# A hybrid decoder block on eight cores: two passes over 512 tokens, or one pass over 1024 with the MLP in two phases

## Chip, cores, metric

One Trainium2 chip, all 8 cores. Each core handles 1024 of the 8192 tokens with all the weights; nothing passes between cores. The metric is device microseconds of the slowest core for one execution. Most executions agree within 0.3%. Some fall in a second, slower state: the four cores of a die (0 to 3 or 4 to 7), or both dies, show a lower granted TensorE clock, and the time is longer. An execution is called slow when one die is over 1% longer than the other at a lower clock, or when it is over 1.5% above the quickest of its kernel. Here fast executions are compared with fast ones. Traces are of fast executions, or of a core on a die that was not disturbed, and then the text says so.

## The reference

```
D_MODEL 4096, BATCH 4, SEQ 2048, one layer;  CONV_WIDTH = GMLP_WIDTH = 2048;  D_FF 16384
xn = rmsnorm(x, mix_norm_g)
b, c, h_in, u, v = split(xn @ w_in)                    # w_in 4096 x 10240
y_a = b * causal_dwconv3(c * h_in)                     # 16 groups of 128 channels
y_b = gelu(u) * (tril(W_s) gelu(v) + bias)             # 16 heads, chunks of 128 positions
h   = x + [rmsnorm(y_a, ga), rmsnorm(y_b, gb)] @ w_out # w_out 4096 x 4096
h   = h + relu(rmsnorm(h, mlp_norm_g) @ w_up)^2 @ w_down   # 4096 x 16384 and back
out = rmsnorm(h, final_norm_g)
```

For one core that is 23,552 matmuls of 128x128 weights against 512 columns, if everything is 512 wide.

## The kernel before

It runs the whole layer twice, for 512 tokens each time, and reads all weights in each pass. The accumulator of 4 x 4096 floats a partition (`acc`) shares its memory with the temporaries of the two mixers. Operations go to per-engine queues, and a helper works out semaphore waits from the buffers that each one reads and writes.

```python
T = 512; NPASS = 2; NSLOT = 4                      # a weight tile: [128, 8192] bf16, 2 MB of bf16, 4 slots; f32 in DRAM

def nt(tt, slot, g_ap, g_buf, extra_w=()):          # norm of 128 tokens, then 32 transposes
    P.op("dve", scalar_tensor_tensor(out=xb, in0=acc[:, tt, :], scalar=stat[:, slot:slot + 1],
                                     in1=g_ap, op0=mult, op1=mult), ...)      # 128 x 4096
    for f4 in range(4):  P.pe([8 transposes of xb, bf16], ...)
    for f4 in range(4):  P.op("dve" or "act", copy psum -> x1, ...)

for ps_ in range(NPASS):
    ...                                             # load x, statistics, nt(): nothing else runs
    def ssq_mm(sq_ap, bsq, first, last):            # sum of squares over channels, for each 128 of them
        P.pe([lambda e: e.matmul(S_bank[:], lhsT=ones_f[:], rhs=sq_ap, start=first, stop=last)], ...)
    ...                                             # input projection + mixers, 20 groups of 256 columns
    P.fence(["sp"], all_tB)                         # acc is free only when the mixers are done
    for tt in range(NTT):
        P.dma("sp", s_x[tt], ... acc[:, tt, :] <- x[r0:r0 + 128, :], writes=B_acc[tt] + all_tB)
    for dc in range(8):                             # out-projection, added onto acc
        for half in range(2):
            slot, bslot = wtile(w_out[dc * 2 + half], v_out)
            ...
    for tt in range(NTT):  stats_fin(4 + tt)
    for tt in range(NTT):  nt(tt, 4 + tt, g2, bg2, ...)
    up_block(0)                                     # 16 blocks of 1024 hidden channels
    for fb in range(NFB):
        if fb + 1 < NFB:  up_block(fb + 1)          # relu, square -> aT in SBUF
        down_block(fb)                              # acc += psum, tensor_tensor on DVE
    ...                                             # final norm, store
# ... (cuts everywhere; operations written short)
```

## Time and profile before

The first three executions took 5658.6, 5661.7 and 5664.6 us; the median is 5661.7. The profiled execution has a span of 5616.7 us.

| stage (slowest core) | us | of it TensorE works |
|---|---|---|
| start of pass 0, start of pass 1 | 92 and 98 | 17 and 14 |
| input projection and mixers | 636 and 608 | nearly all |
| out-projection, with the wait for x before it and the norm after it | 301 and 301 | about 243 each |
| MLP | 1773 and 1775 | all |
| end | 31 | 0 |

Stage limits are the starts of the first large matmul of each kind in the chain of waits, so the stages add up to the span. The names of the engines in all lines: PE is TensorE (matmuls), PEld its weight loads, DVE VectorE, ACT ScalarE, POOL GpSimd, SP SyncE; PEclk is the granted TensorE clock. The lines below are from the page of the kernel before: busy time and share of each engine, three rows of the span cut into 40 slices (tenths), the weights' DMA queue (packets, MB, share), the chain that ended last, and groups of instructions (line, engine, operation, operands, shapes, count, then busy us, mean ns of one, and idle time before them with its cause).

```profile
span 5616.7 us, 62670 instructions; the slowest of 8 cores (5608.2 to 5616.7 us)
...
PE 5281.9 (94%) x25536; PEld 2427.1 (43%) x25536; DVE 1148.9 (20%) x1608; ACT 637.5 (11%) x1232; POOL 196.8 (4%) x374
...
PE   4999979799999999999949999889999999999997
...
PEclk9999989899999999999969999999999999999998
DMA  8887888688888888888589878876888888888885
...
q0 software_dynamic: 52992, 771.78, 77.7%
...
PE 92%; DMA 3%; DVE 3%; ACT 1%; issue 0%; SPq 0%; DVEq 0%; ACTq 0%
...
L660 PE MATMUL ps<-R,ws 128*128 128x512 bf16 x8192 | 1784.7, 379 | 3.0 <-ACT R L390 3.0
L681 PE MATMUL ps<-ws,R 128*128 128x512 bf16 x8192 | 1773.0, 379 | 0.0
...
L619 PE MATMUL ps<-ws,R 128*128 128x512 bf16 x2048 | 456.9, 387 | 55.0 <-DVE R L624 55.0
```

TensorE is busy 94% of the time and on 92% of the chain. L660 and L681 are the two MLP products. No idle time stands before L681, and 3 us before L660. The holes are in the slices: `4`, `7` and `8` at the start, about the middle, and where PEclk falls to 6. L619 is out-projection, with 55 us of idle time before it.

The next lines are stretches (from:to in us, length, busy time of each engine with its instructions, granted clock, DMA share, GB/s).

```profile
core 5: us, PE busy (x) PEld busy (x) DVE busy (x) ACT busy (x) POOL busy (x), PEclk, DMA share, GB/s
0.00:92.00 92.00, 17.14 (x176) 15.89 (x176) 36.98 (x38) 32.65 (x88) 4.75 (x10) 1.00 0.97 214
...
718.00:796.00 78.00, 43.19 (x168) 17.92 (x167) 7.73 (x8) 3.52 (x5) 1.58 (x3) 0.80 0.89 216
...
985.00:1030.00 45.00, 14.69 (x130) 13.56 (x131) 28.82 (x27) 7.05 (x9) 0.53 (x1) 0.58 0.37 87
1030.00:2803.00 1773.00, 1772.98 (x8191) 800.15 (x8189) 353.60 (x511) 173.31 (x318) 65.42 (x124) 1.00 0.82 148
2803.00:2901.00 98.00, 13.89 (x128) 13.04 (x128) 48.44 (x41) 27.18 (x76) 2.11 (x4) 0.53 0.77 226
```

The stretch 1030:2803 is pure matmul at full clock. The others are the losses: a start with 17 us of PE work in 92, a wait for the residual x (718:796), norm and transposes between out-projection and MLP (985:1030) at half the clock, and the start of pass 1.

### The profile page before, as it was taken

How to read it: one execution, taken by the hardware profiler on the slowest of the kernel's cores; microseconds unless marked ns; L12 is line 12 of the kernel's file. 1: busy time of each engine (PE TensorE's matmuls, PEld its weight loads, DVE VectorE, ACT ScalarE, POOL GpSimd, SP SyncE). 2: the span in 40 equal slices, each digit the busy share in tenths (PEclk: the TensorE clock that was granted, in tenths of full speed). 3: DMA queues.
4: the chain of work that ended last, by engine and by line, in shares of the span. 5: the costliest groups of instructions: out<-in, count | busy, mean ns of one | idle time of the engine just before them, and what ended most of it. 6: DMA issues, size and time to landing. Idle time of an engine off the chain costs nothing.

```text
span 5616.7 us, 62670 instructions; the slowest of 8 cores (5608.2 to 5616.7 us)
## 1 busy us (share of the span) xinstructions
PE 5281.9 (94%) x25536; PEld 2427.1 (43%) x25536; DVE 1148.9 (20%) x1608; ACT 637.5 (11%) x1232; POOL 196.8 (4%) x374
## 2 busy tenths in 40 slices
PE   4999979799999999999949999889999999999997
PEld 2444434344444444444424444344444444444443
DVE  2111112212212211221331111121221121122114
ACT  2111101100010001001121111011001000100011
POOL 0000000000000000000000000000000000000000
PEclk9999989899999999999969999999999999999998
DMA  8887888688888888888589878876888888888885
GB/s 180 135 136 129 140 174 154 117 153 153 150 152 152 153 153 152 154 150 152 104 215 159 145 130 146 173 141 128 153 153 152 150 152 152 153 153 152 153 150 135
DMA packets 68553, 840.87 MB, mean 150 GB/s; under 512 B 16690, under 2 KB 16690, under 8 KB 17202
## 3 DMA queue, kind: packets, MB, share of 16 engines
q0 software_dynamic: 52992, 771.78, 77.7%
q1 hardware_dynamic: 14708, 56.70, 3.0%
q10 hardware_dynamic: 576, 8.39, 0.4%
q8 instruction: 212, 3.47, 0.3%
q14 instruction: 65, 0.53, 0.0%
HBM read 1591.81 MB, written 16.78 MB: 286 GB/s over the span
## 4 chain that ended last, share of the span: by engine, by line
PE 92%; DMA 3%; DVE 3%; ACT 1%; issue 0%; SPq 0%; DVEq 0%; ACTq 0%
PE ps L660 32%; PE ps L681 31%; PE ps L459 20%; PE ps L619 7%; DMA R<-x 2%; DVE R L373 1%; PE ps L466 1%; PE ps L381 1%; DVE R L702 1%; DMA R<-mix_g 1%; PE ps L451 0%; DMA R<-xh 0%; DVE R L393 0%; DVE R L473 0%; ACT ps L346 0%
## 5 line engine op out<-in xcount | busy, mean ns | idle before, releaser
L660 PE MATMUL ps<-R,ws 128*128 128x512 bf16 x8192 | 1784.7, 379 | 3.0 <-ACT R L390 3.0
L681 PE MATMUL ps<-ws,R 128*128 128x512 bf16 x8192 | 1773.0, 379 | 0.0
L686 DVE TENSOR_TENSOR R<-ps,R 128x512 f32<-128x512 f32 x1024 | 708.6, 692 | 2843.9 <-PE ps L681 2843.9
L660 PEld LDWEIGHTS ps<-R,ws 128*128 128x128 bf16 x8192 | 799.5, 98 | 983.1 <-issue 5.4
L681 PEld LDWEIGHTS ps<-ws,R 128*128 128x128 bf16 x8192 | 801.5, 98 | 966.6
L459 PE MATMUL ps<-R,ws 128*128 128x512 bf16 x5120 | 1133.5, 380 | 3.4 <-ACT R L390 3.4
L459 PEld LDWEIGHTS ps<-R,ws 128*128 128x128 bf16 x5120 | 496.2, 98 | 621.0 <-issue 38.5
L619 PE MATMUL ps<-ws,R 128*128 128x512 bf16 x2048 | 456.9, 387 | 55.0 <-DVE R L624 55.0
L664 ACT ACTIVATE ps<-ps 128x512 f32<-128x512 f32 x256 | 149.0, 582 | 3004.6 <-PE ps L660 3004.6
L619 PEld LDWEIGHTS ps<-ws,R 128*128 128x128 bf16 x2048 | 203.4, 100 | 307.9 <-issue 75.8
L381 PE MATMUL ps<-ident_b,R 128*128 128x128 bf16 x512 | 56.8, 309 | 173.1 <-DVE R L373 173.1
L624 DVE SCALAR_TENSOR_TENSOR R<-ps,inv_tok,R 128x512 f32<-128x512 f32 x128 | 95.0, 750 | 417.8 <-PE ps L619 289.7
L666 ACT ACTIVATE R<-ps 128x512 bf16<-128x512 f32 x256 | 152.8, 597 | 23.9 <-ACT ps L664 0.7
L352 ACT ACTIVATE ps<-R 128x512 f32<-128x512 f32 x128 | 76.9, 601 | 653.9 <-DVE R L624 478.0
L506 DVE TENSOR_TENSOR R<-ps,R 128x512 f32<-128x512 f32 x32 | 22.1, 692 | 598.5 <-PE ps L459 598.5
L251 POOL DMA_DIRECT2D ws<-w_up x128 | 67.5, 527 | 1793.1 <-PE ps L681 1472.1
L381 PEld LDWEIGHTS ps<-ident_b,R 128*128 128x128 bf16 x512 | 53.0, 145 | 177.4 <-issue 177.4
L251 POOL DMA_DIRECT2D ws<-w_down x128 | 67.6, 528 | 1710.2 <-PE ps L660 1587.8
L251 POOL DMA_DIRECT2D ws<-w_in x80 | 42.4, 530 | 1296.5 <-PE ps L459 820.7
L565 DVE COPY R<-ps 128x512 bf16<-128x512 bf16 x32 | 13.6, 425 | 334.9 <-PE ps L561 334.9
L373 DVE SCALAR_TENSOR_TENSOR R<-R,stat 128x4096 bf16<-128x4096 f32 x16 | 71.7, 4481 | 14.0 <-DMA R<-mix_g 13.2
L466 PE MATMUL ps<-R,ones_f 128*128 128x512 f32 x128 | 68.3, 616 | 3.5 <-ACT R L586 3.5
(64 smaller groups left out, 682.0 us busy)
## 6 DMA issues: line engine op xcount, KB each, us to landing
ws<-w_up POOLq DMA_DIRECT2D x128, 2048.0 KB, 14.6
ws<-w_down POOLq DMA_DIRECT2D x128, 2048.0 KB, 14.5
ws<-w_in POOLq DMA_DIRECT2D x80, 2048.0 KB, 16.0
ws<-w_out POOLq DMA_DIRECT2D x32, 2048.0 KB, 15.4
R<-x SPq DMA_DIRECT2D x12, 2048.0 KB, 17.9
out<-R SPq DMA_DIRECT2D x8, 2048.0 KB, 8.5
R<-x ACTq DMA_DIRECT2D x4, 2048.0 KB, 17.4
R<-mix_g SPq DMA_DIRECT2D x2, 2048.0 KB, 32.4
```

The costliest lines, as they stand in the source:

```text
L251: P.dma("pool", s_slot[s], lambda e: e.dma_start(out=flat, in_=src_ap), writes=[B_slot[s]])
L373: P.op("dve", lambda e: e.scalar_tensor_tensor(out=xb, in0=src, scalar=stat[:, slot:slot + 1], in1=g_ap, op0=ALU.mult, op1=ALU.mult), read ...
L381: fns.append(lambda e, i=i, c=c, bank=bank: e.transpose(out=bank[:, i * 128:(i + 1) * 128], in_=xb[:, c * 128:(c + 1) * 128], identity=ide ...
L459: fns.append(lambda e, kc=kc, bank=bank: e.matmul(bank[:], lhsT=slot[:, kc, i * 128:(i + 1) * 128], rhs=x1[:, kc, 2:514], start=(kc == 0), ...
L466: P.pe([lambda e: e.matmul(S_bank[:], lhsT=ones_f[:], rhs=sq_ap, start=first, stop=last)], reads=[bsq, B_const], writes=[B_S])
L619: fns.append(lambda e, cc=cc, bank=bank, tt=tt, half=half, slot=slot: e.matmul(bank[:], lhsT=yT[:, half * 16 + cc, tt * 128:(tt + 1) * 128 ...
L624: P.op("dve", lambda e, bank=bank, dst=dst, tt=tt, half=half: e.scalar_tensor_tensor(out=dst, in0=bank[:], scalar=inv_tok[:, half * 4 + tt ...
L660: fns.append(lambda e, kc=kc, bank=bank, slot=slot, i=i: e.matmul(bank[:], lhsT=slot[:, kc, i * 128:(i + 1) * 128], rhs=x1[:, kc, 2:514], ...
L664: P.op("act", lambda e, bank=bank: e.activation(out=pst[3][:], in_=bank[:], func=AF.Relu), reads=[bb], writes=[B_ps[3]])
L666: P.op("act", lambda e, fb=fb, fcl=fcl: e.activation(out=aT[fb % 2][:, fcl, :], in_=pst[3][:], func=AF.Square), reads=[B_ps[3]], writes=[B ...
L681: fns.append(lambda e, fc=fc, bank=bank, slot=slot, tt=tt, dcl=dcl, fb=fb: e.matmul(bank[:], lhsT=aT[fb % 2][:, fc, tt * 128:(tt + 1) * 12 ...
L686: P.op("dve", lambda e, bank=bank, dst=dst: e.tensor_tensor(out=dst, in0=bank[:], in1=dst, op=ALU.add), reads=[bb, B_acc[tt][dc]], writes= ...
```

## The change

Its intent: read each weight once. All 1024 tokens stay in memory as the transposed activation `XT`. They are transposed *before* the norm, with the norm's gain applied as the psum (the memory that takes TensorE's results) is copied out. The token factor 1/rms, which only scales a column of the product, is multiplied in when the product is read. The first six products already run while x arrives ("k-outer"). The MLP becomes two phases: all of up, whose 33.5 MB of activations go to DRAM, then all of down. The factor for `relu(.)^2`, 1/ms, is applied as down is accumulated. h goes to DRAM and back since its memory is needed. Sums of squares are added up on DVE.

```diff
-T = 512 ... NPASS = 2 ... FB = 1024
+TOK = 1024
+NT = 8
+NFULL = 15
+        h_d = nc.dram_tensor("h_d", [8, 128, 4096], F32).ap()
+        a_d = nc.dram_tensor("a_d", [DFF // 128, 128, TOK], BF16).ap()
-        slots = [sb("ws%d" % i, [128, 8192], BF16) for i in range(NSLOT)]
+        slots = [sb("ws%d" % i, [128, 4096], BF16) for i in range(NSLOT)]
 ... # start: transposes of raw x in f32, and six products fed as blocks of x come in
+        for db in range(9):
+            for u in range(8):
+                if db < 8:
+                    ... P.pe(4 f32 transposes) ; evac_t(XT[...], bnk[:], g1[:, kc:kc + 1], ...)
+                    ... P.act(Square of xst, accum_out=statp[...])
+                if db > 0:
+                    kouter((db - 1) * 4 + u // 2, range((u % 2) * 3, (u % 2) * 3 + 3))
 ... # the token norm on the psum read
+            P.dve(lambda e: e.tensor_tensor(out=z, in0=bnk[:], in1=inv_bc[:, 2 + p * 512:514 + p * 512],
+                                            op=ALU.mult), reads=[bb, B_inv], writes=[bz])
 ... # c and h_in with their two halo columns: three pieces of 342 columns
+            for p in range(3):
+                bnk, bb = in_piece(sl, bsl, p * 342, 342)
 ... # sums of squares on DVE
-                P.pe([lambda e: e.matmul(S_bank[:], lhsT=ones_f[:], rhs=sq_ap, start=first, stop=last)], ...)
+                    P.dve(lambda e, sa=sa, sq_=sq_: e.tensor_tensor(out=sa, in0=sa, in1=sq_, op=ALU.add), ...)
 ... # out-projection: h is transposed in f32 among its matmuls and stored to DRAM
+                            defer(3, lambda db=db: x2_part(db, 0, (0, 1)))
+            P.dma("sp", s_hs[db % 2], ... h_d[db] <- a)
 ... # up, then down
+        for f in range(DFF // 128):
+            ... 2 x 32 matmuls, relu, square -> at
+            P.dma("sp", s_aT[f % 3], lambda e, f=f, at=at: e.dma_start(out=a_d[f], in_=at), ...)
+        for f in range(NFULL):
+            ... acc = psum * inv2m + acc  (scalar_tensor_tensor), a tile of 8 matmuls
+        ... # last 1024 channels in two halves, tiles of 4 matmuls, the second half with sums of squares and final norm
 ... # (cuts everywhere)
```

## The prediction

> **What bounds the kernel now.** TensorE. The page puts PE at 94% of the 5616.7 us span, and the chain of waits is 92% PE. In the two MLP stretches (windows 1030–2803 and 3811–5585) PE is busy 1773 of 1773 us at granted clock 1.00, 215.8 ns a 128x512 matmul in down and 217.1 in up (chain pieces 55.25 and 55.57 us for 256). That agrees with the Trainium skill, "TensorE: Matmul & The Clock Gate", section "Back-to-back issue gap" (N/2.4 + 2.5 ns = 215.8). DMA is 82% busy there but nothing waits for it. So weight traffic is not the bound; only the some 530 us outside the 23552 large matmuls (5083 us at 215.8) can be won.
>
> Where these lie (windows, chain, timeline): start of pass 0, 92 us; start of pass 1, 98; both without large matmuls. Wait for the residual x before out-projection, about 42 us twice (78 us windows with 168 matmuls). Norm and transposes between out-projection and MLP, 45 us twice at clock 0.58. Ones-matmuls in f32 for the sums of squares (L466), 64 x 0.87 = 56 us. Halo products (L451), 25 us. Norm extraction inside the input projection, 6 us twice. End, 31 us.
>
> **What the change does.**
> - Weights are read once, DMA bytes for weights halve (772 to 386 MB), about 100 MB of h and activations are added. Off the path: 0 us either way.
> - One start instead of two. 16.8 MB of x at the 214 GB/s of the first window, plus three weight tiles: about 110 us (estimate), but 192 matmuls (41 us) run inside it. Saves 120.
> - Residual x is loaded under the end of the conv stage and h goes out and back in the background: saves 84.
> - The norm moves onto the psum reads, x is transposed under out-projection: saves 90 less about 3 of bubble, but 256 f32 transposes are put between the matmuls, 0.11 to 0.22 us each (four took 1.09 us after an idle stretch, at L477): costs 28 to 56.
> - Ones-matmuls become DVE adds: saves 56. Halo columns go into 342-wide pieces: saves 25, and 1024 more matmul instructions of the conv stage cost some 4 us by the same 2.5 ns; DVE stays far below PE.
> - Up reads an aligned activation tile: it may run at 215.8 rather than 217.1 ns, 0 to 10 us.
> - End: the last half of down does 4-matmul tiles (0.86 us) with a square (0.8 us on ACT), an add (0.7 us on DVE), and the final norm; ACT and DVE become the limit, some 70 to 75 us of work against 55 of PE, then the last store. Tail about 33 us, no gain.
>
> **Sum of stages after (estimate):** start 110, gating heads 420, conv 672, out-projection 485, up 1770, down 1768, tail 33, bubbles 8: span 5266 to 5290. The time before lies 45 us above its span; so 5320 us.
>
> **Predicted: 5320 us, range 5280 to 5390.** Faster by over 2%: 0.96; within 2%: 0.03; slower: 0.01.
>
> **What would show it.** MLP stages still 3536–3547 us together with no PE gap and clock 1.00; no wait for x before out-projection; no stretch at clock 0.5 to 0.6 in mid-kernel; PE share about 97 to 98%; DMA share about 45%; conv stage about 670 us; start about 110 us; between out-projection and up a gap below 5 us; f32 transposes 60 us or less in out-projection.
>
> **What would make it wrong.** A lower granted clock under one unbroken dense stream. A start bound by the two transposing banks or by ACT squares rather than DMA (to 140 us). Costlier f32 transposes or switches between f32 and bf16 (another 50 us). Activations coming late from DRAM at the start of down. A tail above 50 us.

## The result, and the profile after

Six executions of the changed kernel: 5272.2, 5268.6 and 5267.6 us fast, 5520.7, 5723.8 and 5890.7 us slow. In the slow ones one die had a clock of 0.88 to 0.95 and the other ran its usual 5259 to 5268 us. The median of all six, 5396 us, says little about the kernel. The kernel before took 5640.5, 5660.3 and 5615.7 us in these rounds; with the first three that makes its first six. The ratio of fast runs to those of before was 0.9326 (95% interval 0.9282 to 0.937), on a later visit 0.9381 (0.9364 to 0.9397). Such a ratio is the mean time of one kernel's fast runs over that of the other's in the same rounds, so it is not quite the ratio of the medians that I quote.

So the kernel is 6 to 7% faster. The predicted 5320 us is 51 us too high, and the fast runs lie below the range (5280 to 5390); the median lies above it.

The same lines of the page, of the changed kernel (L803 is up, L843 down but for its last 1024 channels):

```profile
span 5270.5 us, 61915 instructions; the slowest of 8 cores (5257.8 to 5270.5 us)
...
PE 5179.0 (98%) x25401; PEld 2480.1 (47%) x25401; DVE 1250.5 (24%) x1706; ACT 619.9 (12%) x1144; POOL 241.5 (5%) x391
...
PE   6999999999999999999999999999999999999997
...
PEclk8999999999999999999999999999999999999998
DMA  6544434345555664444444444464444445444454
...
q0 software_dynamic: 54288, 385.90, 40.5%
...
PE 98%; another core or an unknown queue 0%; DMA 0%; issue 0%; DVE 0%; ACT 0%; POOLq 0%; DVEq 0%; ACTq 0%
...
L803 PE MATMUL ps<-AB,ws 128*128 128x512 bf16 x8192 | 1768.3, 379 | 0.0
L843 PE MATMUL ps<-ws,TT 128*128 128x512 bf16 x7680 | 1657.8, 379 | 0.0
```

TensorE is at 98%, and the slices show one hole only, the first. The weights' queue moved half the bytes. Stretches by stage, with the same columns; the last one starts where the tiles of 4 matmuls do:

```profile
0.00:130.40 130.40, 79.57 (x470) 53.85 (x471) 39.11 (x66) 55.36 (x153) 9.82 (x20) 0.90 0.68 171
...
1220.00:1692.80 472.80, 471.73 (x2321) 230.89 (x2320) 113.32 (x156) 74.17 (x173) 17.41 (x33) 1.00 0.54 132
1692.80:3460.90 1768.10, 1768.10 (x8193) 801.57 (x8192) 0.48 (x3) 313.56 (x512) 67.06 (x127) 1.00 0.51 104
3460.90:5118.50 1657.60, 1657.60 (x7682) 751.47 (x7680) 719.71 (x959) 1.23 (x2) 63.33 (x120) 1.00 0.49 100
5118.50:5270.50 152.00, 114.42 (x512) 50.24 (x510) 116.54 (x153) 61.50 (x144) 42.52 (x13) 0.91 0.53 160
```

| stage | before | after, predicted | after, measured | gained |
|---|---|---|---|---|
| start(s) | 190.6 | 110 | 130.4 | 60.2 |
| input projection, mixers | 1244.6 | 1092 | 1089.4 | 155.2 |
| out-projection and its gaps | 601.9 | 485 | 472.9 | 129.0 |
| MLP matmuls | 3548.3 | 3538 | 3536.2 | 12.1 |
| end | 31.3 | 33 | 41.5 | -10.2 |
| bubbles | in the stages | 8 | in the stages | |
| span | 5616.7 | 5266 | 5270.5 | 346.2 |

"End" after is the last stretch, 152.0 us, less its 512 matmuls at 215.8 ns (110.5 us). The predicted *span*, 5266 to 5290 us, holds the measured 5270.5. What failed is what I added to it.

### The profile page after: what moved, and what is told of

Same layout as the page of the kernel before. It is cut to its first block, busy times and chain, and to the rows that moved or that the text cites. A ratio compares the mean times of both kernels' runs of the same rounds, so it can differ in the third digit from the quotient of the medians.

```text
span 5270.5 us, 61915 instructions; the slowest of 8 cores (5257.8 to 5270.5 us)
## 1 busy us (share of the span) xinstructions
PE 5179.0 (98%) x25401; PEld 2480.1 (47%) x25401; DVE 1250.5 (24%) x1706; ACT 619.9 (12%) x1144; POOL 241.5 (5%) x391
## 4 chain that ended last, share of the span: by engine, by line
PE 98%; another core or an unknown queue 0%; DMA 0%; issue 0%; DVE 0%; ACT 0%; POOLq 0%; DVEq 0%; ACTq 0%
PE ps L803 34%; PE ps L843 31%; PE ps L531 20%; PE ps L744 8%; PE ps L865 2%; PE ps L436 1%; PE ps L449 1%; PE ps L726 1%; DMA AB<-x 0%; ACT TT L831 0%; PE ps L566 0%; PE ps L582 0%; DVE AB L826 0%; POOLq L925 0%
## 5 line engine op out<-in xcount | busy, mean ns | idle before, releaser
L803 PE MATMUL ps<-AB,ws 128*128 128x512 bf16 x8192 | 1768.3, 379 | 0.0
L843 PE MATMUL ps<-ws,TT 128*128 128x512 bf16 x7680 | 1657.8, 379 | 0.0
L826 DVE SCALAR_TENSOR_TENSOR AB<-ps,stat,AB 128x512 f32<-128x512 f32 x1088 | 813.2, 750 | 2715.4 <-PE ps L843 2705.5
L803 PEld LDWEIGHTS ps<-AB,ws 128*128 128x128 bf16 x8192 | 801.6, 98 | 966.3
L843 PEld LDWEIGHTS ps<-ws,TT 128*128 128x128 bf16 x7680 | 751.5, 98 | 906.1
L531 PE MATMUL ps<-AB,ws 128*128 128x342 bf16 (+1 forms) x5952 | 1074.8, 342 | 1.0 <-DVE TT L541 1.0
L531 PEld LDWEIGHTS ps<-AB,ws 128*128 128x128 bf16 x5952 | 574.0, 97 | 488.2 <-issue 4.0
L744 PE MATMUL ps<-ws,AB 128*128 128x512 bf16 x2048 | 447.2, 379 | 0.0
L809 ACT ACTIVATE TT<-ps 128x512 f32<-128x512 f32 x256 | 152.8, 597 | 1419.1 <-PE ps L803 1419.1
L744 PEld LDWEIGHTS ps<-ws,AB 128*128 128x128 bf16 x2048 | 200.4, 98 | 234.7
L811 ACT ACTIVATE TT<-TT 128x512 bf16<-128x512 f32 x256 | 161.0, 629 | 35.6 <-DMA a_d<-TT 4.7
L865 PE MATMUL ps<-ws,TT 128*128 128x512 bf16 x512 | 114.6, 386 | 13.1 <-DVE AB L826 13.1
L865 PEld LDWEIGHTS ps<-ws,TT 128*128 128x128 bf16 x512 | 50.4, 99 | 77.1 <-issue 19.5
L755 ACT ACTIVATE TT<-TT 128x512 bf16<-128x512 f32 x64 | 40.3, 630 | 323.2 <-DVE TT L751 323.2
```

What stands on the lines that cost most here:

```text
L531: fns.append(lambda e, kc=kc: e.matmul(bnk[:, 0:n], lhsT=slot[:, kc * 128:(kc + 1) * 128], rhs=XT[:, kc, lo:lo + n], start=(kc == 0), stop ...
L744: fns.append(lambda e, cc=cc, bnk=bnk, t=t, half=half, ss=ss: e.matmul(bnk[:], lhsT=yT[:, half * 16 + cc, t * 128:(t + 1) * 128], rhs=ss[c ...
L803: fns.append(lambda e, kc=kc, bnk=bnk, p=p, sl=sl: e.matmul(bnk[:], lhsT=sl[:, kc * 128:(kc + 1) * 128], rhs=X2[:, kc, p * 512:(p + 1) * 512],
L809: P.act(lambda e, bnk=bnk, r_=r_: e.activation(out=r_, in_=bnk[:], func=AF.Relu), reads=[bb], writes=[br])
L811: P.act(lambda e, r_=r_, p=p, at=at: e.activation(out=at[:, p * 512:(p + 1) * 512], in_=r_, func=AF.Square), reads=[br], writes=[bat])
L826: P.dve(lambda e: e.scalar_tensor_tensor(out=acc[:, b, t, :], in0=bnk[:], scalar=inv2m[:, t:t + 1], in1=acc[:, b, t, :], op0=ALU.mult, op1 ...
```

## The experiments

Eleven kernels, on three visits, each to another chip. In each visit they share the executions of the kernel before, which took 5617.9, 5619.3 and 5618.1 us undisturbed; so close are the chips that times of different visits are compared below. The changed kernel was run again in the first visit only, where it took 5269.5 us. Times are means of fast runs unless stated.

### The offset, and the traffic

The unchanged kernels again, the kernel before with half the weight bytes, and the changed kernel with twice as many.

> The kernel before, unchanged, to see the spans and clocks of the cores of every run. Theory O (a fixed offset of about 45 us between the time and the span of the slowest core, as the prediction assumed): every run's time lies about 45 us above the span of its slowest core. Theory V (the profiled execution was simply a quick one, the offset is about 2 us and the spans themselves vary): time minus the slowest span is under 5 us in every run, and the slowest spans scatter between 5615 and 5665 us. Under V the clocks tell more: with the clock equal (0.97 to 0.975) in quick and long runs the extra time is waiting; with a lower clock in long runs it is throttling.

> The changed kernel again, to have it in the same rounds. All theories: fast runs at 5265 to 5275 us, time minus slowest span under 5 us; some runs in the slow state with one die at a clock of 0.88 to 0.95.

Seven of the executions, from the per-core record (us; clock as mean of the die's cores):

```
kernel, execution           time      slowest core   die 0 spans / clock       die 1 spans / clock
before, fast                5617.5    5615.9         5605-5615 / 0.975         5610-5616 / 0.975
before, fast                5620.1    5618.6         5612-5619 / 0.975         5608-5614 / 0.974
before, called fast         5657.7    5656           5631-5656 / 0.969         5608-5618 / 0.975
before, slow                5690.1    5688           5612-5615 / 0.974         5678-5688 / 0.960
before, slow                6583.2    6582           6566-6582 / 0.818         5606-5613 / 0.975
changed, fast               5268.0    5266           5261-5266 / 0.995         5260-5266 / 0.995
changed, slow               5371.7    5370           5261-5266 / 0.995         5364-5370 / 0.974
```

Time minus the slowest core's span is 1.5 to 1.7 us in every execution of every kernel. That holds for the changed kernel's first six too, which ran in the same rounds as the last three of the first six before. There is no offset of 45 us: theory O falls. V has the offset right; its scatter of spans from 5615 to 5665 us did not come. The third row (from the second visit) shows where such a time can come from: at 5657.7 us die 1 ran as ever, and the cores of die 0 were 18 to 43 us longer than the usual 5613, at a clock lower by 0.006. The first executions of the kernel before, on which the prediction stood, have no per-core record. That they were such executions is therefore not shown directly; but of 35 executions of that kernel with a record, 16 lie between 5616.4 and 5620.2 us, 18 are slow (5690 and more), and this one is the only one between; and the quickest of the first six was 5615.7. Against it speaks that five of those six lie at 5640 to 5665 us, where only one of the 35 later ones does: the first rounds differed from the later ones by something that is not on record. Undisturbed, the kernel before takes 5618 us and the changed one 5269.5, a ratio of 0.938; the prediction's own ratio, 5320 to 5661.7, was 0.940.

> The kernel before with half of every weight tile loaded (the first four tiles whole, wrong result on purpose); all matmuls, waits and the other loads stay. Theory M (the kernel before sits near the limit of the memory that 8 cores share, and its typical run waits for weights now and then; so halving the weight traffic was worth something by itself): fast runs at 5560 to 5620 us, 40 us or more below the kernel before in the same rounds, and a narrow scatter. Theory C (the long runs of the kernel before come from the granted clock, not from memory): no difference beyond 15 us. The prediction said 0 us for the traffic.

```diff
-            P.dma("pool", s_slot[s], lambda e: e.dma_start(out=flat, in_=src_ap), writes=[B_slot[s]])
+            nc_ = 8192 if n < NSLOT else 4096
+            P.dma("pool", s_slot[s], lambda e: e.dma_start(out=flat[:, 0:nc_], in_=src_ap[:, 0:nc_]),
+                  writes=[B_slot[s]])
```

Its output is wrong, which doesn't matter for the time. One execution of seven was fast, at 5580.5 us, against 5617.9 for the kernel before: 37 us less, just under what theory M wanted, and far from the prediction's zero. It did not come from MLP, where nothing had waited. It came from the gaps: the stage from the first out-projection matmul to the first up matmul took 282 us in pass 0 and 281 in pass 1, against 301 and 301, and the starts stayed as they were (93 and 97 us). The residual x, which shares the DMA engines with prefetched weights, arrives sooner. The out-projection group of the page, to compare with L619 of before (55.0 us of idle time there):

```profile
L621 PE MATMUL ps<-ws,R 128*128 128x512 bf16 x2048 | 452.5, 385 | 21.2 <-DVE R L626 21.2
```

> The changed kernel with every weight tile but the first three loaded twice, the second load issued after that of the next tile, so weight traffic is that of the kernel before; no wait for the second load should show if memory keeps up (it has some 28 us of slack). Theory M: fast runs 30 us or more above the changed kernel, more scattered, with waits of PE for weight loads in the trace. Theory C: within 15 us of the changed kernel. Neither theory expects the granted clock to differ in fast runs.

```diff
+        def load(s, src):  ... P.dma("pool", s_slot[s], ...)
         def wtile(src):
-            P.dma("pool", s_slot[s], lambda e: e.dma_start(out=flat, in_=src), writes=[B_slot[s]])
+            load(s, src)                       # tile n
+            if last:  load(*last.pop())        # tile n-1 once more
+            last.append((s, src))
 ...
-            want(i + 1)
+            want(i + 3)
```

5680 us in five fast runs, 410 above the changed kernel: waits as theory M has them, but far more than the traffic alone explains. The waits of TensorE told why: 256 us of them stood before out-projection's matmuls. That stage takes tiles in pairs, and with my order of issue the second load of a pair's later tile was issued only when the pair before was done. That part is an artefact of the edit. The next run leaves those tiles single.

> The changed kernel with all weight tiles but those of out-projection and the first three loaded twice. In the earlier doubling, 256 us of waits fell in out-projection, where tiles are taken in pairs and my order of issue made each pair wait for its second load; that was an artefact of the edit. Theory Z (the prediction's: weight traffic of the old size is off the path, also beside the activations in DRAM): within 20 us of the changed kernel, 5265 to 5290. Theory M (it costs, since the DMA engines get to 90% and tiles come late): 5310 to 5370, with waits of up and down matmuls for weight loads.

```diff
-            last.append((s, src))
+            if not 80 <= n < 112:              # not w_out
+                last.append((s, src))
```

5377.1 us (four fast runs): 107 us above the changed kernel, just over theory M's range, and the result is correct. Theory M holds, my zero falls. Up and down as stretches, then TensorE's waits (who waited for what: us in total, times, longest):

```profile
1707.00:3531.80 1824.80, 1778.14 (x8195) 803.45 (x8194) 0.68 (x4) 312.86 (x512) 134.45 (x255) 0.99 0.99 175
3531.80:5205.30 1673.50, 1662.55 (x7682) 752.48 (x7681) 719.84 (x959) 1.23 (x2) 126.56 (x240) 1.00 0.97 174
```

```profile
PE ps L813 <- DMA ws<-w_up: 24.3, 5, 8.0
PE ps L813 <- ACT TT L819: 22.4, 1, 22.4
...
PE ps L853 <- DMA ws<-w_down: 10.9, 2, 6.7
```

The DMA engines are 97 to 99% busy. Up took 1824.8 us, where it took 1768.1, and down's first part 1673.5 in place of 1657.6; the start and the last stretch took 14 and 16 us more, the other stages the same. Tiles come late (24.3 us), and ACT is held up once by 22.4 us in a stage where its own output must be stored before its buffer is free. The Trainium skill, "HBM Reference", section "Specifications (TRN2)", gives about 358 GB/s of effective bandwidth for each core of a pair. The page of this run counts 302 GB/s read and written on average over the span, the kernel before 286, the changed one 176. The weights are f32 in DRAM and bf16 when they land, so each byte in the weights' queue is two bytes read (771.78 MB in the queue of the kernel before, 1591.81 MB read). An estimate for MLP from that: before, 537 MB of weights in 1773 us are 303 GB/s, and PE waited for none; here, up moved 535 MB of weights and 33.5 MB of activations in 1824.8 us, 311 GB/s, and PE waited. So the traffic of before was close to what could be had here; whether the memory or the DMA engines set that limit, no run separates. In the kernel before the traffic cost 37 us in the gaps and nothing in MLP. In the new structure, with h and the activations going through DRAM as well, nearly the same traffic (734 MB in the weights' queue, since out-projection's tiles stay single) costs 107. A part of this can still be the edit: a tile loaded twice must be complete within some 28 us, by the expectation of the first doubling, and that lead was not varied. Halving the traffic is what lets that structure hold.

### Parts of the change, alone, on the kernel before

> The kernel before without its two kinds of mid-kernel gaps: the residual x isn't loaded before out-projection (the accumulator keeps what was in that memory) and the norm and transposes between out-projection and MLP are left out (MLP reads the old normed x); wrong result on purpose, all large matmuls stay. Theory G (the gaps are pure loss on the chain and were worth 84 and 90 us, as the prediction costed them): fast runs 165 to 180 us below the kernel before, that is 5437 to 5452 us. Rival W (with the gaps gone the same weights must come in less time and PE waits for them, the loads being 82 to 89% of the DMA time): less than 130 us, with new waits of PE for weight loads.

```diff
-            P.dma("sp", s_g, ... g2stage <- mlp_g, writes=all_x1)
-            P.fence(["sp"], all_tB)
-            for tt in range(NTT):
-                P.dma("sp", s_x[tt], ... acc[:, tt, :] <- x, writes=B_acc[tt] + all_tB)
+            P.fence(["dve"], all_tB)
 ...
-            P.op("act", lambda e: e.copy(out=gbc, in_=g2stage), ...)
-            for tt in range(NTT):  stats_fin(4 + tt)
-            for tt in range(NTT):  nt(tt, 4 + tt, g2, bg2, ...)
+            P.fence(["act", "sp"], [B_yT])
```

5466.3 us in three fast runs; the kernel before had two undisturbed ones in these rounds, 5618.4 and 5620.2 (the ratio of fast runs, 0.9706, counts the 5657.7 as well). That is 153 us, between the theories' numbers, but rival W's new waits for weights are not in the trace. The time from the first out-projection matmul to the first up matmul of a pass shrank from 301.1 and 300.8 us to 223.5 and 222.9: 155 us, all of the gain. So the gaps are pure loss, and the cost was cut out wrongly: the window of 78 us in which I read 42 us of waiting for x begins at 718, but the first out-projection matmul starts at 728.5. The 10 us before it hold 7.7 us in which PE waits for the conv mixer's last square (1.7 us) and its norm extraction (5.9). That is no wait for x, and this edit leaves it in place. It is 15 us of the 19 that are missing over both passes.

> The kernel before with one part of the change alone: sums of squares added up on DVE, one ones-matmul for each mixer and pass instead of 16. Theory S (the f32 ones-matmuls sit in PE's order and each costs its 0.87 us): 50 to 56 us below the kernel before, 5561 to 5567 us. Rival (DVE's adds hold up its reads of the products and PE waits for banks): less than 30 us.

```diff
-                P.pe([lambda e: e.matmul(S_bank[:], lhsT=ones_f[:], rhs=sq_ap, start=first, stop=last)], ...)
+                if first: P.op("dve", ... tensor_copy(out=sqacc, in_=sq_ap), ...)
+                else:     P.op("dve", ... tensor_tensor(out=sqacc, in0=sqacc, in1=sq_ap, op=ALU.add), ...)
+                if last:  P.pe([lambda e: e.matmul(S_bank[:], lhsT=ones_f[:], rhs=sqacc, start=True, stop=True)], ...)
```

5567.2 us, correct: 52 us less than those two undisturbed runs, as theory S had it. The edit removes 60 of the 64 ones-matmuls, 52 us at 0.87: here the work moved from TensorE to an engine with room was gained in full.

### Terms that were mis-sized in the changed kernel, and a kernel from them

The start took 20 us more than predicted on the slowest core (119 to 130 us on the eight, 125 on average). The chain of waits of the changed kernel (start us, us, what) shows the first transposes at 23.6 us and then a long wait, which the view of waits puts down to the load of x:

```profile
23.64 1.10 PE ps L449 x4
...
31.02 21.71 another core or an unknown queue
52.97 1.09 PE ps L449 x4
```

Twelve quarter tiles of weights and 1 MB of spatial weights share the DMA engines with the first two blocks of x.

> The changed kernel with the start's loads in another order: of the three first weight tiles only the first quarter is loaded at once, the other quarters and the spatial weights after x blocks 0, 2 and 3 have landed. Theory D (the start took 130 us and not the predicted 110 since x shares the DMA engines with weights that nobody needs yet; blocks landed at 23.6 and 52.9 us): first block before 18 us, second before 35, start stage 105 to 115 us, fast runs 15 to 25 us below the changed kernel. Rival P (the start is set by PE's and the readers' 8.7 us for a block of x): under 6 us gained.

```diff
-        P.dma("act", s_misc["spw"], ... spw_f <- sp_w)
         for q in range(4):
+            if q > 0:
+                P.wait("pool", B_xst[(0, 2, 3)[q - 1]].w)     # after x block 0, 2, 3
+            if q == 2:
+                P.dma("pool", s_misc["spw"], ... spw_f <- sp_w)
             for s in range(3):
                 ...
-            if db in (2, 3):                                   # transposes of the spatial weights
+            if db in (5, 6):
```

5262.0 us in two fast runs, 7.5 below the changed kernel's 5269.5 (from another visit), half of what theory D wanted. The profile fell on a slow execution; the lines are of core 4, on the die that was not disturbed (timeline: start us, us, engine, line, operation, operands, shapes, count, idle before and its cause):

```profile
17.53 1.94 PE L452 MATMUL ps<-ident_f,AB 128*128 128x128 f32 x8 [11.03 <-DMA AB<-x]
...
28.46 1.08 PE L452 MATMUL ps<-ident_f,AB 128*128 128x128 f32 x4 [3.39 <-DMA AB<-x]
...
66.41 1.09 PE L452 MATMUL ps<-ident_f,AB 128*128 128x128 f32 x4 [7.41 <-DMA AB<-x]
...
81.37 1.09 PE L452 MATMUL ps<-ident_f,AB 128*128 128x128 f32 x4 [3.95 <-DMA AB<-x]
```

The blocks now land at 17.5 and 28.5 us, in the expected bounds, and the start on this core ends at 117 us, not 130. But x blocks later on make PE wait 7.4 and 3.9 us: a part of the load was moved, not removed. And the cores of the changed kernel differ: up started between 1680.3 and 1692.6 us on its eight cores (mean 1686.2), with the edit between 1676.1 and 1679.9 on the four of the undisturbed die (mean 1678.1). So the 130 us are those of a late core, and the edit's worth is 8 us on average. Theory D has the cause right and the size too large by half.

The end: the last stretch works in tiles of four matmuls, 0.86 us each.

> The changed kernel with the last stage's sums of squares tracked by token group (a reduction no longer waits for the newest square of the next group) and the final norm split in two steps with two tiles between. Theory T (the last stage is 152 us against 110 of matmuls because DVE stands 1.8 us in each token group waiting for ACT, while its adds back up and PE runs out of banks): 10 to 14 us below the changed kernel, the period of a token group 9.5 us before and about 8 after. Rival A (ACT's squares and scaling are the limit themselves): under 4 us gained.

```diff
-                      ... writes=[junk2[b % 2][1]], cols=[B_statp])
+                      ... writes=[junk2[b % 2][1]], cols=[B_stt[t]])      # one buffer for each token group
-        def finish(t):
+        def finish1(t):
             ... reduce_sum, sqrt
+        def finish2(t):
             ... reciprocal, scale, gain, store
-                defer(4, lambda t=t: finish(t))
+                defer(3, lambda t=t: finish1(t))
+                defer(5, lambda t=t: finish2(t))
```

5263.6 us in three fast runs: 6 us gained, between the theories' bounds. DVE's timeline in the changed kernel, an operation of the second token group and then one whole group:

```profile
5201.99 3.48 DVE L899 SCALAR_TENSOR_TENSOR AB<-AB,stat,TT 128x2048 f32<-128x2048 f32 x1
...
5227.94 0.16 DVE L883 TENSOR_REDUCE stat<-statp 128x1 f32<-128x8 f32 x1 [0.97 <-ACT TT L831]
5228.50 0.16 DVE L887 RECIPROCAL stat<-stat 128x1 f32<-128x1 f32 x1 [0.40 <-ACT stat L885]
5228.88 2.35 DVE L899 SCALAR_TENSOR_TENSOR AB<-AB,stat,TT 128x2048 f32<-128x2048 f32 x1 [0.21 <-DVE stat L887]
...
5237.47 0.16 DVE L883 TENSOR_REDUCE stat<-statp 128x1 f32<-128x8 f32 x1 [0.97 <-ACT TT L831]
```

and with the edit:

```profile
5199.75 5.75 DVE L902 SCALAR_TENSOR_TENSOR AB<-AB,stat,TT 128x2048 f32<-128x2048 f32 x1
...
5223.88 0.15 DVE L884 TENSOR_REDUCE stat<-statp 128x1 f32<-128x8 f32 x1
5223.95 1.40 DVE L827 SCALAR_TENSOR_TENSOR AB<-ps,stat,AB 128x512 f32<-128x512 f32 x2
...
5225.52 2.35 DVE L902 SCALAR_TENSOR_TENSOR AB<-AB,stat,TT 128x2048 f32<-128x2048 f32 x1
...
5231.74 0.15 DVE L884 TENSOR_REDUCE stat<-statp 128x1 f32<-128x8 f32 x1
```

Before the edit DVE stands 0.97 us for ACT's newest square and 0.40 for the square root; the period is 5237.47 - 5227.94 = 9.53 us. With it, no wait for ACT is left but in the last group, and the period is 5231.74 - 5223.88 = 7.86. The mechanism of theory T is right. The gain is half, for a reason that no run isolated but the first line suggests: in the second and third group the same 128x2048 operation takes 5.75 and 4.97 us, not 2.35. It was slow there in the changed kernel too, but less: 3.48 and 3.41 us. That is 3.8 us lost of the 10 that theory T wanted at least. GpSimd's timeline, with the edit, has its products there, back to back:

```profile
5198.81 17.61 POOL L899 TENSOR_TENSOR AB<-AB,TT 128x2048 f32<-128x2048 f32 x3 [23.80 <-ACT stat L886]
```

The Trainium skill, "SBUF — State Buffer", section "Who interferes with whom", says that a DVE instruction with two SBUF inputs contends with a GpSimd instruction that reads SBUF, and that the second to start is held up. Both are such operations here, GpSimd's began first (5198.81 against 5199.75 us), and 5.75 us against 2.35 agrees.

The transposes among out-projection's matmuls. The chain of the changed kernel, eight f32 transposes (L726) between matmuls:

```profile
1269.91 0.87 PE ps L726 x8
1270.78 3.45 PE ps L744 x16
1274.23 0.87 PE ps L726 x8
```

> The changed kernel with the transposes under out-projection in bf16: ACT first copies each finished tile of h to bf16. In the trace four f32 transposes take 0.435 us between matmuls, 27.8 us in 64 groups. If the f32 transposes cost what they show (0.109 us each) and bf16 ones half (four in 0.22 us, as in the gating stage of the kernel before): out-projection 14 us shorter, fast runs 5253 to 5258 us. Rival: ACT's copies hold up the stage, and nothing is gained (within 3 us).

```diff
+                        P.act(lambda e, t=t, a=a: e.copy(out=hb[:, t, :], in_=a[:, t, :]), ...)   # h to bf16
-                        in_=a[:, g * 4 + i, c * 128:(c + 1) * 128], identity=ident_f[:]))
+                        in_=hb[:, g * 4 + i, c * 128:(c + 1) * 128], identity=ident_b[:]))
```

The same lines with the edit (core 4, the slowest of that run):

```profile
1265.42 0.45 PE ps L730 x8
1265.87 3.45 PE ps L748 x16
1269.32 0.45 PE ps L730 x8
```

Eight f32 transposes took 0.87 us, 109 ns each, at the low end of my 0.11 to 0.22; eight in bf16 take 0.45. The stage went from 472.9 to 460.8 us. Three fast runs gave 5257.8 us, 11.7 less (a fourth, 5296.5, is called fast but has a die at a clock of 0.986 to 0.991; it is left out here, and the ratio of fast runs, 0.9383, counts it). Expected was 14.

> The changed kernel with three edits together: loads of the start reordered (spatial weights now after x block 5, since in the earlier version their small packets seem to have held up block 4 by 7 us), sums of squares of the last stage tracked by token group, bf16 transposes under out-projection. If they add: 8 to 15 us, 6 to 7 us and 14 us, so fast runs at 5232 to 5242 us. If they hide one another: over 5245 us.

The edit is the three above, with the spatial weights' load moved further back, after x block 5. Correct; 5233.6 and 5234.4 us in two fast runs of eight, against 5618.1 for the kernel before in the same rounds: ratio 0.9317, 95% interval 0.9295 to 0.934. It beats both kernels, and the edits add as forecast: 35.5 us less than the changed kernel. Alone they had given 7.5, 6 and 11.7, 25 us together. Most of the other 10 is in the start, where this run differs from the first reordering: in its trace (core 4 of the die left alone) the start ends at 108.4 us, not 117.

## Why the prediction was wrong, point by point

- **The bound, and the size of the gain: right.** TensorE at 98%, MLP at full clock without a gap, no stretch at half clock in mid-kernel. The stage sum of 5266 us met a span of 5270.5.
- **The step that failed: "The time before lies 45 us above its span; so 5320 us."** It took the difference between three timed executions and another, profiled one for a property of the measurement. The offset is 1.5 to 1.7 us in all executions with a record. The typical undisturbed kernel before takes 5618 us. Predicted from the span with that offset, the time would have been 5268 to 5292 against the measured 5269. A possible source of the 45 us was seen in one execution of that size (5657.7 us, one die at a clock lower by 0.006); for the first executions themselves the cause remains open, as they have no per-core record.
- **"Off the path: 0 us either way": wrong.** It was read from MLP alone, where nothing waited. Half the traffic in the kernel before gave 37 us (one fast run), in the waits for x, which my items had counted under that name; nearly the old traffic in the new structure cost 107 us in four fast runs, a part of it perhaps by the shorter lead. The change does halve the traffic and loads x early, so the sum came out right all the same.
- **Start 110 us: mis-sized**, measured 130.4 on the slowest core, 125 on average. The estimate took the DMA engines as the limit throughout. In the run the second block of x came late, behind weights that nobody needed yet, and after it PE worked at its own 8.7 us a block. Reordering brought 117 us, and 108 with the spatial weights later.
- **Waits for x and mid norms, 174 us: 155 measured.** The window for x held some 7.5 us a pass of waits for the last square and the norm extraction, which are not waits for x.
- **Ones-matmuls, 56 us: 52 measured,** with four of the 64 left in. f32 transposes, 28 to 56: about 28 measured.
- **End 33 us: 41.5 measured.** The right engines were named. The second half of the last stretch took 97 us (5173.7 to 5270.5), 42 more than its 55 of matmuls; I had 70 to 75 us of work and the last store. DVE's waits for ACT (1.4 us of each group) and GpSimd in DVE's way in the second and third group weren't in it.
- **Up at 215.8 ns for a matmul: right in number, reason open.** L803 took 1768.3 us for 8192. I had put it down to an aligned activation tile; but the new input projection reads with the same two-column shift as before and runs at 215.8 as well (13.81 us for 64), so alignment alone doesn't explain it. No run took this apart. Nor did any take apart the rest of the input projection's 155 us: products done in the start (41), sums of squares (52), halo (25), the four norm extractions (24, the waits of L477 in the trace before; I had listed two of them, 12) and the 1.3 ns on each of 5120 matmuls (7) come to 149 by estimate.
- **Granted clock: right for fast runs.** That three of the first six executions fell in the slow state is not explained here, and the kernel before falls there too.

## What to carry to other kernels

Before a predicted span is turned into a time, compare times and spans of the *same* execution, core by core: a difference between executions is not an offset. A stage in which nothing waits says that its traffic fits, not that the traffic is free elsewhere: look at what else wants the DMA engines at the starts and gaps. When PE is the bound, count its idle stretches once, by stage limits that add up to the span, and check every item of a list against that table.

## What the Trainium skill lacked or had wrong

- "TensorE: Matmul & The Clock Gate", section "Seeing it yourself": it says that three or more dense cores on a die bring a 13/16 clock within about 5 to 20 us, held while the load lasts, and to budget for that. Here all 8 cores ran dense matmuls on random data for 1773 us at a granted clock of 1.00 in fast executions. The state exists: the longest slow execution of the kernel before had one die at 0.818 (13/16 is 0.8125) and 6583 us; but most slow ones had means between, and the other die was often untouched. It can end while the load goes on: in the profiled slow execution of the reordered start, core 1 shows 0.81 in every stretch of 800 us up to 4000 us and 1.00 from 4800 to 5600, with PE busy 800 of 800 us in most of them.
- The same page, section "PE-mode transpose": it gives the length of one bf16 transpose, about 390 ns alone and 275 in one kernel, and nothing for f32 or for how closely they follow each other. Among matmuls at full clock they were 219 ns long in bf16 and 273 in f32 (medians of 256), and eight in a row took 0.45 us (56 ns each) and 0.87 us (109 ns each).
- "HBM Reference": it says that with both cores of a pair streaming each gets about its share of 358 GB/s. Here tiles came late at some 311 GB/s with the DMA engines 99% busy (up of the doubled kernel), and none did at 303 (MLP before); both are estimates from bytes and stage times. The page has no rate for loads that turn f32 into bf16 on the way, beside stores.
- "SBUF — State Buffer", section "Who interferes with whom": agrees; it gives no size for a float `scalar_tensor_tensor` against a GpSimd `tensor_tensor`. Here 3.41 to 5.75 us in place of 2.35 for 128x2048.
